# Rotary keys and queries: half-heads in two column tiles instead of 32-row swapped reads, in a hybrid Fourier and windowed-attention encoder

## The chip, the cores and the metric

One core of a Trainium2 chip runs the whole kernel. The metric is the device time of one execution in microseconds (us); of several runs the median counts. The kernel before takes 2726.4 us (median of three, 2724.59 to 2726.91).

## The reference, cut to what matters

One encoder layer on two batches, 512 and 256 positions, which share all weights; the kernel treats them as T = 768 columns. D is 2048. The part that the change touches is the projection `z = h @ w_in`, the rotation of q and k, and the way into the attention:

```python
h = rmsnorm(x, ln_mix_g)
z = h @ w_in                      # 2048 -> 1024 fourier | 1024 q | 256 k | 256 v
of = fourier_mix(zf, w_fourier)   # 8 groups x 128 channels: Re(2-D DFT), then a map per group
def apply_rope(x, cos, sin):      # x: (B, S, heads, 64)
    half = HEAD_DIM // 2
    x1, x2 = x[..., :half], x[..., half:]
    rot = jnp.concatenate([-x2, x1], axis=-1)
    return x * c + rot * s        # c, s: cos and sin per position, the same for all heads
q = apply_rope(q, cos, sin); k = apply_rope(k, cos, sin)   # 16 q heads, 4 k heads
oa = window_attention(q, k, v, attn_sink)   # each token sees +-128 positions, sink logit per head
x = x + concat([rmsnorm(of), rmsnorm(oa)]) @ w_out
x = x + relu(rmsnorm(x) @ w_up)**2 @ w_down            # then a final rmsnorm
```

All data are float32. TensorE takes a rounded form, so each operand is split in a high and a low part and each product is made of three matmuls (high x high, high x low, low x high). "Split" below means: ScalarE (ACT) writes the high part, VectorE (DVE) subtracts it from the source and writes the low part.

## The kernel before, in words

The stages follow one another on TensorE (PE): transposing and norming x, the v projection, the Fourier group's projection, then a stage that we call the pieces, then attention interleaved with the output projection, then the MLP, which is two thirds of the time.

The stage of the pieces makes the columns of k and q. There are five pairs of 256 columns (`cols`), and each pair is four pieces of 512 rows of `w_in`: 20 pieces, 0 to 19, of 48 matmuls each. Pair 0 holds the four key heads; pairs 1 to 4 hold query groups 0 to 3 (four heads that share a key head). A piece's weights come by a 512 KB load on SP's queue (`wload`, L79) into `raw`, two buffers; `split` makes `wh` (L69, ACT) and `wl` (L70, DVE). A pair's products lie in four PSUM tiles `pz` (L818), which is all there are: the next pair's first matmul waits until ACT has copied the tiles out (`zs`, L826). While PE works on pieces 0 to 10, the other engines carry out the Fourier group's DFT steps; `todo` holds work that is emitted after a certain piece or half piece.

The rotation goes by DRAM. ACT copies a pair's result to `zs`, writes it to `zk_d` or `zq_d` in three writes: 64 rows per head, and again its first 32 rows as rows 64 to 95. `rows2` reads rows 0 to 63 of two heads as `rx` and rows 32 to 95 as `ry`, in two halves of 384 positions, so `ry` has the halves of the heads swapped. Such a read stands in the code as

```python
nc.sync.dma_start(out, src[:, d : d + 64, t0])     # 2 heads x 64 rows x 384 positions
```

`rotate` (L677 on POOL, L678 and L679 on DVE) gives x cos + y sin. `keys` splits the rotated keys into `kdh`, `kdl` (L695, L697), which hold each key group in both halves of the partitions. `queries` splits the rotated queries into `rh`, `rl` (L72, L73) and writes them to DRAM (`qr_d`, L710, L711). 16 such jobs (4 for keys, 12 for query groups 0 to 2) are queued at pieces 10 to 18, and group 3 is read back and rotated in the attention.

Attention has 24 units (6 blocks of 128 positions x 4 groups). `load_q` reads a unit's queries from DRAM into `rx` (L723, L724), `split_q` copies them to `qs` (L740), and PE makes the scores `s` (L862) from `kdh`, `kdl` and `qs`. Between them lie matmuls of the output projection (`pm`, L1051, L1053). The order there is a list of events with times in steps of one eighth of a projection slot, units 7.37 steps apart (`pace`); the engines' queues are laid out in that order. Up to the end of piece 18 the queues of ACT, DVE, POOL and SP get their order from a scheduler, and PE's order is that of the code.

Of the kernel before, what the change touches and what calls it, by code (L numbers as in the profile page):

```python
# [20 lines left out]
P = 128  # L21
# [19 lines left out]
def hybrid_encoder(ctx: ExitStack, tc: tile.TileContext, a: dict):  # L41
# [74 lines left out]
    zk_d = [dpool.tile([2, 96, T], F32, tag=f"zk{i}", name=f"zk{i}") for i in range(2)]  # L116
    zq_d = [dpool.tile([4, 96, T], F32, tag=f"zq{i}", name=f"zq{i}") for i in range(NKV)]
    qr_d = [[dpool.tile([2 * P, T], F32, tag=f"q{c}{i}", name=f"q{c}{i}") for c in "hl"] for i in range(NKV - 1)]
# [79 lines left out]
    with ExitStack() as ph:  # L198
# [339 lines left out]
        zp = ph.enter_context(tc.tile_pool(name="zp", bufs=2, reuse_waits="tile"))  # L538


# [107 lines left out]
        def fourier_norm():  # L648
            ps_r = pp.tile([P, 512], F32, tag="f", bufs=4, name="ps_r")
            for m in range(NM):  # L650
                nc.tensor.matmul(ps_r[:, m : m + 1], ssf[:, m * P : (m + 1) * P], ones[:, 0:1], start=True, stop=True)
            rsqrt_of(r1[:], ps_r[:, :NM], FG * P, NM)
            fctx.close()


        kt = {}

        def open_attention():
            kp = kt["kp"] = kctx.enter_context(tc.tile_pool(name="kp", bufs=1, side="right", reuse_waits="tile"))
            for name, shape, src in (  # L660
                ("mask", [P, 384], a["c_mask"]), ("cosr", [P, T], a["c_cos"]), ("sinr", [P, T], a["c_sin"]),
                ("sink", [P, 64], a["attn_sink"].partition_broadcast(P)),
            ):
                kt[name] = kp.tile(shape, F32, tag=name, name=name)
                nc.sync.dma_start(kt[name][:, : src.shape[1]], src)
            for name in ("cosr", "sinr"):
                nc.vector.tensor_tensor(out=kt[name][:], in0=kt[name][:], in1=rb[:], op=ALU.mult)
            kt["kdh"] = kp.tile([P, NKV, T], F32R, tag="kdh", name="kdh")
            kt["kdl"] = kp.tile([P, NKV, T], F32R, tag="kdl", name="kdl")

        def rotate(x, y, t0, engine=nc.gpsimd):

            shape = x.shape
            cb, sb = (
                kt[c][: shape[0], t0].rearrange("p (o t) -> p o t", o=1).to_broadcast(shape) for c in ("cosr", "sinr")
            )
            engine.tensor_tensor(out=y, in0=y, in1=sb, op=ALU.mult)  # L677
            nc.vector.tensor_tensor(out=x, in0=x, in1=cb, op=ALU.mult)  # L678
            nc.vector.tensor_tensor(out=x, in0=x, in1=y, op=ALU.add)  # L679

        def rows2(src, t0):

            x, y = (kt["kp"].tile([P, 1, 512], F32, tag=c, name=c, bufs=n)[:, :, :HALF] for c, n in (("rx", 2), ("ry", 2)))
            for out, d in ((x, 0), (y, 32)):
                nc.sync.dma_start(out, src[:, d : d + 64, t0])
            return x, y

        def keys(i, t0, x, y):
            rotate(x, y, t0)
            x = x[:, 0, :]  # L690
            kdh, kdl = kt["kdh"], kt["kdl"]
            for r in range(2):
                g, rs = 2 * i + r, slice(r * HD, (r + 1) * HD)
                for h in (slice(0, 64), slice(64, 128)):
                    nc.scalar.activation(kdh[h, g, t0], x[rs], AF.Copy)  # L695
                for h in (slice(0, 64), slice(64, 128)):
                    nc.vector.tensor_tensor(out=kdl[h, g, t0], in0=x[rs], in1=f32(kdh[rs, g, t0]), op=ALU.subtract)  # L697

        def queries(g, i, t0, x, y):

            rs = slice(i * P, (i + 1) * P)
            rotate(x, y, t0)
            x = x[:, 0, :]
            if g < 2:
                hi = kt["kp"].tile([P, 512], F32R, tag="qs", name="rh", bufs=2)[:, :HALF]
            else:
                hi = kt["kp"].tile([P, HALF], F32R, tag="rl", name="rh", bufs=2)[:]
            lo = kt["kp"].tile([P, HALF], F32, tag="rl", name="rl", bufs=2)
            split(hi, lo[:], x, HD ** -0.5)
            nc.scalar.dma_start(qr_d[g][0][rs, t0], f32(hi))  # L710
            nc.scalar.dma_start(qr_d[g][1][rs, t0], lo[:])  # L711
# [4 lines left out]
        def load_q(u):  # L716
            b, g = units[u]
            t0 = slice(b * P, (b + 1) * P)
            x = kt["kp"].tile([P, 4, P], F32, tag="rx", name="rx", bufs=2)
            state[u] = {"x": x}  # L720
            if g < NKV - 1:
                rows = lambda src: src[:, t0].rearrange("(h d) t -> d h t", d=HD)
                nc.sync.dma_start(x[0:64], rows(qr_d[g][0]))  # L723
                nc.sync.dma_start(x[64:128], rows(qr_d[g][1]))  # L724
                return
            y = kt["kp"].tile([P, 4, P], F32, tag="ry", name="ry", bufs=2)
            for out, d in ((x, 0), (y, 32)):
                nc.sync.dma_start(out[0:64], zq_d[g][:, d : d + 64, t0].rearrange("h d t -> d h t"))
            state[u]["y"] = y

        def rotate_q(u):
            b, g = units[u]
            if g == NKV - 1:
                rotate(state[u]["x"][:HD], state[u].pop("y")[:HD], slice(b * P, (b + 1) * P), nc.vector)

        def split_q(u):
            x = state[u].pop("x")
            qs = state[u]["qs"] = kt["kp"].tile([P, 4, P], F32R, tag="qs", name="qs", bufs=2)
            if units[u][1] < NKV - 1:
                nc.scalar.activation(qs[:], x[:], AF.Copy)  # L740
                return
            nc.scalar.activation(qs[0:64], x[0:64], AF.Copy, scale=HD ** -0.5)
            nc.vector.scalar_tensor_tensor(
                out=qs[64:128], in0=x[0:64], scalar=HD ** -0.5, in1=f32(qs[0:64]), op0=ALU.mult, op1=ALU.subtract
            )
# [16 lines left out]
        jobs = [(keys, (i,), zk_d[i][:], s) for i in range(2) for s in range(2)]  # L762
        jobs += [(queries, (g, i), zq_d[g][2 * i : 2 * i + 2], s) for g in range(NKV - 1) for i in range(2) for s in range(2)]
        got = {}

        def job_load(i, src, s):
            got[i] = rows2(src, slice(s * HALF, (s + 1) * HALF))

        for i, (fn, args, src, s) in enumerate(jobs):
            t = 10.5 + 0.5 * i  # L770
            after(t - 0.5, lambda i=i, src=src, s=s: job_load(i, src, s))
            after(t, lambda i=i, fn=fn, args=args, s=s: fn(*args, slice(s * HALF, (s + 1) * HALF), *got.pop(i)))
        for u in range(2):
            after(18.5 + 0.5 * u, lambda u=u: (load_q(u), split_q(u)))
        after(18.5, lambda: load_of(0, [kt["kp"].tile([P, 4, P], F32, tag="ry", name="ofr", bufs=2) for _ in range(2)]))
        dst = [zk_d[i][:] for i in range(2)]
        dst += [zq_d[i // 2][i % 2 * 2 : i % 2 * 2 + 2] for i in range(8)]
        cols = [2048, 1024, 1280, 1536, 1792]
# [11 lines left out]
        def piece_split(p):  # L790
            if p < n_in:
                in_w[p] = wsplit(in_raw.pop(p))
# [11 lines left out]
        for piece in range(n_in):  # L804
            pair, j = divmod(piece, 4)
            if piece == 19:
                last.enter_context(tc.manual_schedule(engines={mybir.EngineType.Activation, mybir.EngineType.DVE}))
# [4 lines left out]
            for c in range(2):  # L812
# [9 lines left out]
                if j == 3:  # L822
                    zs = zp.tile([P, T], F32, tag="zs", name="zs")
                    for s in range(2):
                        hs = slice(s * HALF, (s + 1) * HALF)
                        nc.scalar.copy(zs[:, hs], ps[c][s][:, :HALF])  # L826
                    queue, to = nc.gpsimd if piece == n_in - 1 else nc.scalar, dst[2 * pair + c]
                    queue.dma_start(to[:, :64], zs[:])
                    for r in range(2):
                        queue.dma_start(to[r, 64:], zs[64 * r : 64 * r + 32])  # L830
# [8 lines left out]
        last.close()  # L839
# [160 lines left out]
    t_w, t_of, t_xc, t_y, t_oa, t_oa0, t_oa1, t_rot, t_split = 42.05, 7.45, -0.05, 2.7, 67, 4.2, 4.95, 5.8, 9  # L1000
# [15 lines left out]
    for u in range(len(units)):  # L1016
# [53 lines left out]
    with tc.manual_schedule(engines={mybir.EngineType.SP, mybir.EngineType.Activation, mybir.EngineType.DVE, mybir.EngineType.Pool}):  # L1070
# [14 lines left out]
        run_events(1e9)  # L1085
    att.close()
# [673 lines left out]
def _constants():  # L1760
# [20 lines left out]
        "c_cos": f(np.concatenate([c, c, c, c], 0)),  # L1781
        "c_sin": f(np.concatenate([-sn, sn, -sn, sn], 0)),
# [33 lines left out]
```

## Time and profile before

| | us |
|---|---|
| median of three runs | 2726.4 |
| profiled execution, its own time | 2724.45 |
| its span | 2722.7 |
| PE busy in the span | 2588.2 (95%) |
| DVE busy | 1805.1 (66%) |
| ACT busy | 1123.4 (41%) |
| POOL busy | 255.0 (9%) |
| PE busy from 300 to 503: pieces 11 to 19, up to the first score | 87.15 of 203 |

The profiled execution takes 1.75 us beyond its span. In the rows of the trace the times are microseconds from the start of the span; a row of PE's timeline has the start, the length, and in brackets the idle time ahead of it and what ended that. "<-" between two tile names reads "made from". SPq is the queue of SyncE, in which loads stand in order: a load that waits for a free buffer holds up all loads behind it.

### The profile page before, as it was taken

How to read it: one execution, taken by the hardware profiler on the slowest of the kernel's cores; microseconds unless marked ns; L12 is line 12 of the kernel's file. 1: busy time of each engine (PE TensorE's matmuls, PEld its weight loads, DVE VectorE, ACT ScalarE, POOL GpSimd, SP SyncE). 2: the span in 40 equal slices, each digit the busy share in tenths (PEclk: the TensorE clock that was granted, in tenths of full speed). 3: DMA queues.
4: the chain of work that ended last, by engine and by line, in shares of the span. 5: the costliest groups of instructions: out<-in, count | busy, mean ns of one | idle time of the engine just before them, and what ended most of it. 6: DMA issues, size and time to landing. Idle time of an engine off the chain costs nothing.

```text
span 2722.7 us, 35114 instructions
## 1 busy us (share of the span) xinstructions
PE 2588.2 (95%) x13580; PEld 2366.8 (87%) x13580; DVE 1805.1 (66%) x2230; ACT 1123.4 (41%) x1613; POOL 255.0 (9%) x359
## 2 busy tenths in 40 slices
PE   9999735599999999999999999999999999999998
PEld 9999735488888999999999999988888888888887
DVE  7955221577775655655677777767775774777687
ACT  6534210477643333333344444443333333333335
POOL 1002200222421010100000000020000000000000
PEclk9999867799999999999999999999999999999999
DMA  7954222534457445445666666686553481555264
GB/s 255 312 199 132 88 85 92 180 115 130 159 191 237 152 166 180 171 148 204 226 213 221 230 214 222 213 304 230 172 181 117 157 302 57 174 179 175 85 209 155
DMA packets 270008, 492.30 MB, mean 181 GB/s; under 512 B 20641, under 2 KB 164561, under 8 KB 268689
## 3 DMA queue, kind: packets, MB, share of 16 engines
q1 hardware_dynamic: 200624, 322.84, 36.9%
q10 hardware_dynamic: 55216, 115.18, 11.2%
q0 software_dynamic: 14000, 52.05, 5.6%
q8 instruction: 106, 1.74, 0.3%
q14 instruction: 62, 0.50, 0.1%
HBM read 361.92 MB, written 128.06 MB: 180 GB/s over the span
## 4 chain that ended last, share of the span: by engine, by line
PE 89%; DMA 7%; DVE 2%; SPq 0%; issue 0%; POOL 0%; ACT 0%; DVEq 0%; POOLq 0%; ACTq 0%
PE pu L1197 34%; PE pd L1632 33%; PE pm L1051 8%; PE p L268 4%; PE pz L818 3%; DMA rx<-zq 3%; DMA ry<-zq 2%; PE pv L391 1%; DMA ry<-zk 1%; PE s L862 1%; PE t L919 1%; PE o L938 1%; DMA rx<-zk 1%; PE pe L633 0%; PE pa L612 0%
## 5 line engine op out<-in xcount | busy, mean ns | idle before, releaser
L1197 PE MATMUL pu<-xf,wh 128*128 128x384 f32 x3072 | 780.2, 334 | 0.0
L1197 PEld LDWEIGHTS pu<-xf,wh 128*128 128x128 f32 x3072 | 553.9, 188 | 1.5 <-ACT o L1215 1.3
L1632 PE MATMUL pd<-wl,sh 128*128 128x512 f32 x1332 | 517.7, 389 | 0.0
L1632 PE MATMUL pd<-wh,sh 128*128 128x512 f32 x1332 | 517.7, 389 | 0.0
L1632 PE MATMUL pd<-wh,sl 128*128 128x512 f32 x1332 | 517.5, 389 | 0.0
L1197 PE MATMUL pu<-xf,wl 128*128 128x384 f32 x1536 | 513.1, 334 | 0.0
L1609 ACT ACTIVATE wh<-rd 128x1024 fp32r<-128x1024 f32 x200 | 202.4, 1054 | 522.2 <-PE pd L1632 414.3
L1619 DVE TENSOR_TENSOR wl<-rd,wh 128x1024 fp32r<-128x1024 f32 x200 | 236.1, 1221 | 226.3 <-ACT wh L1609 225.6
L1177 ACT ACTIVATE wh<-ur 128x1024 fp32r<-128x1024 f32 x160 | 170.0, 1063 | 382.5 <-PE pu L1197 207.4
L1632 PEld LDWEIGHTS pd<-wh,sl 128*128 128x128 f32 x1332 | 249.9, 188 | 52.1 <-DVE sl L1620 0.3
L1632 PEld LDWEIGHTS pd<-wl,sh 128*128 128x128 f32 x1332 | 250.0, 188 | 51.9
L1632 PEld LDWEIGHTS pd<-wh,sh 128*128 128x128 f32 x1332 | 250.0, 188 | 51.6
L1197 PEld LDWEIGHTS pu<-xf,wl 128*128 128x128 f32 x1536 | 288.3, 188 | 0.0
L1183 DVE TENSOR_TENSOR wl<-ur,wh 128x1024 fp32r<-128x1024 f32 x160 | 195.4, 1221 | 75.8 <-ACT wh L1177 75.7
L1218 DVE TENSOR_TENSOR o<-pu,o 128x768 f32<-128x768 f32 x160 | 152.8, 955 | 122.8 <-PE pu L1197 114.9
L1602 DVE TENSOR_TENSOR rd<-rd 128x1024 f32<-128x1024 f32 x112 | 131.7, 1217 | 0.0
L1197 PE MATMUL pu<-xs,wh 128*128 128x384 f32 x512 | 129.8, 334 | 0.0
L818 PE MATMUL pz<-xf,wh 128*128 128x384 f32 x320 | 72.5, 349 | 58.5 <-ACT zs L826 58.5
L1177 ACT ACTIVATE wh<-sx 128x1024 fp32r<-128x1024 f32 x64 | 67.9, 1062 | 130.5 <-PE pu L1197 104.3
L268 PE MATMUL p<-xs,wh 128*128 128x384 f32 x448 | 113.9, 334 | 0.0
L818 PEld LDWEIGHTS pz<-xf,wh 128*128 128x128 f32 x320 | 58.8, 197 | 59.5 <-ACT zs L826 59.3
L1620 DVE TENSOR_TENSOR sl<-sr,sh 128x768 fp32r<-128x768 f32 x111 | 105.5, 950 | 0.0
(283 smaller groups left out, 3970.8 us busy)
## 6 DMA issues: line engine op xcount, KB each, us to landing
rd<-in_w_down SPq DMA_DIRECT2D x176, 512.0 KB
ur<-in_w_up SPq DMA_DIRECT2D x128, 512.0 KB
sr<-sd SPq DMA_DIRECT2D x95, 384.0 KB
pd<-o ACTq DMA_DIRECT2D x60, 384.0 KB
o<-pd POOLq DMA_DIRECT2D x60, 384.0 KB, 6.0
sd<-sm ACTq DMA_DIRECT2D x60, 384.0 KB
raw<-in_w_in SPq DMA_DIRECT2D x38, 512.0 KB
raw<-in_w_out SPq DMA_DIRECT2D x32, 512.0 KB
```

The lines of the kernel that those rows point to most:

```text
L268: nc.tensor.matmul(ps7[bank, g, r][:, :HALF], l[:, i, r * P : (r + 1) * P], x[:, o, 4 * e + i, :], start=(opens and e == 0 and i == 0 and ...
L818: nc.tensor.matmul(ps[c][s][:, :HALF], w[:, i, cs], whole[j // 2][s][o][:, 4 * (j % 2) + i, :], start=first and n == 0, stop=stop and n == 2,)
L1051: nc.tensor.matmul(ps, l(k), w[:, k % 2, :], start=(k == 0 and n == 0), stop=(k == 7 and n == 2))
L1177: nc.scalar.activation(wh[:], raw[:], AF.Copy)
L1183: nc.vector.tensor_tensor(out=wl[:], in0=raw[:], in1=f32(wh[:]), op=ALU.subtract)
L1197: nc.tensor.matmul(ps[:, t, :HALF], w[:, i, t * P : (t + 1) * P], xb[:, o, i, :], start=(s == first_of[bank] and i == 0 and n == 0), stop= ...
L1218: nc.vector.tensor_tensor(out=o, in0=src, in1=o, op=ALU.add)
L1602: add = lambda x, y, op: nc.vector.tensor_tensor(out=x[:], in0=x[:], in1=y[:], op=op)
L1609: nc.scalar.activation(wh[:], t[:], AF.Copy)
L1619: nc.vector.tensor_tensor(out=wl[:], in0=t[:], in1=f32(wh[:]), op=ALU.subtract)
L1620: nc.vector.tensor_tensor(out=sl[:], in0=sr[:], in1=f32(sh[:]), op=ALU.subtract)
L1632: nc.tensor.matmul(o, l[:, q, ts], w[:, ns], start=(j == j0 and (q, t) == (0, 0)), stop=(j == j1 and (q, t) == (1, 2)),)
```

## The change

The weight columns of a pair are permuted when the pieces are split: the high and low parts are written with the column order (d, head) instead of (head, d). So column tile c = 0 of a pair (128 rows of the product) holds the first halves of its four heads, and c = 1 the second halves, at the same row. Then the swapped partner of a row lies in the other tile on the same partition, and rotation needs no swapped read: z0 cos - z1 sin, z1 cos + z0 sin. The tables `c_cos` and `c_sin` are laid out accordingly.

The order of the pairs is now keys, group 2, group 0, group 1, group 3 (`cols`, `order`). Pairs 0 and 1 still go by DRAM (`zs_d`, one write for each tile, one read of 768 KB). Pairs 2, 3 and 4 are copied from PSUM straight into the tile that is rotated. The rotation works in three steps of 256 positions (`cross` on POOL, `turned` on DVE, `parts` on ACT and DVE), and the high and low parts of keys and queries are written to `kr_d` and `qr_d`. The keys come back by four loads of 768 KB (`load_k`); `load_q` reads the queries straight into `qs`, without the copy by ACT. Pair 4 is rotated in the attention's events, and a unit's queries are loaded 1.5 steps after the time of the unit two before it (`t_lq`).

```diff
-        jobs = [(keys, (i,), zk_d[i][:], s) for i in range(2) for s in range(2)]
-        jobs += [(queries, (g, i), zq_d[g][2 * i : 2 * i + 2], s) for g in range(NKV - 1) for i in range(2) for s in range(2)]
...
-        cols = [2048, 1024, 1280, 1536, 1792]
+        cols = [2048, 1536, 1024, 1280, 1792]
+        order = [None, 2, 0, 1, 3]
+        for pair, t, ahead in ((0, 10.5, 10), (2, 11.5, None), (1, 13, 12), (3, 15, None)):
+            if ahead is not None:
+                after(ahead, lambda pair=pair: load_z(pair))
+            for s in range(3):
+                after(t + s // 2 * 0.5, lambda pair=pair, s=s: cross(pair, s))
+                after(t + 0.5 + s // 2 * 0.5, lambda pair=pair, s=s: (turned(pair, s), parts(pair, s)))
+        after(13, load_k)
...
+        def z_tile(pair):
+            zt[pair] = (zo["p"] if pair in (2, 3) else kt["kp"]).tile([P, 2, T], F32, tag="zs", name="zs")
+
+        def load_z(pair):
+            z_tile(pair)
+            nc.sync.dma_start(zt[pair][:], zs_d[pair][:].rearrange("(b p) t -> p b t", p=P))
+
+        def cross(pair, s):
+            ts = slice(s * 256, (s + 1) * 256)
+            y = ys[pair, s] = kt["kp"].tile([P, 2, 256], F32, tag="zy", name="zy", bufs=2)
+            for b in range(2):
+                nc.gpsimd.tensor_tensor(out=y[:, b], in0=zt[pair][:, 1 - b, ts], in1=kt["sinr"][:, ts], op=ALU.mult)
+
+        def turned(pair, s):
...
+            nc.vector.tensor_tensor(out=z, in0=z, in1=cb, op=ALU.mult)
+            for b, op in enumerate((ALU.subtract, ALU.add)):
+                nc.vector.tensor_tensor(out=z[:, b], in0=z[:, b], in1=y[:, b], op=op)
+
+        def parts(pair, s, when=lambda dt, fn: fn()):
...
+            put = lambda o, x: nc.scalar.dma_start(out[o][:, ts].rearrange("(b p) t -> p b t", p=P), x)
...
+                nc.scalar.activation(hi[:], z, AF.Copy, scale=scale)
+                low = lambda: nc.vector.scalar_tensor_tensor(
+                    out=z.bitcast(F32R), in0=z, scalar=scale, in1=f32(hi[:]), op0=ALU.mult, op1=ALU.subtract
+                )
+            put(0, f32(hi[:]))
+            when(t_zl, low)
+            when(t_zp, lambda: put(1, z))
+
+        def load_k():
+            for o, c in enumerate(("kdh", "kdl")):
+                for h in (slice(0, HD), slice(HD, P)):
+                    nc.sync.dma_start(f32(kt[c][h]), kr_d[o][:].rearrange("(d h) t -> d h t", h=NKV))
...
-            x = kt["kp"].tile([P, 4, P], F32, tag="rx", name="rx", bufs=2)
+            qs = kt["kp"].tile([P, 4, P], F32R, tag="qs", name="qs", bufs=2)
+            for o in range(2):
+                nc.sync.dma_start(f32(qs[o * HD : (o + 1) * HD]), qr_d[g][o][:, t0].rearrange("(d h) t -> d h t", h=4))
...
-                in_w[p] = wsplit(in_raw.pop(p))
+                raw = in_raw.pop(p)
+                wh, wl = in_w[p] = [wpool.tile([P, 4, 256], F32R, tag=f"w{c}", name=f"w{c}", bufs=4) for c in "hl"]
+                hi, lo = (w[:].rearrange("p i (d h) -> p i h d", h=4) for w in (wh, wl))
+                split(hi, lo, raw[:].rearrange("p i (h d) -> p i h d", h=4))
...
-            at(t - 3, lambda u=u: load_q(u + 2))
-            at(t - 3 + t_rot, lambda u=u: rotate_q(u + 2))
-            at(t - 3 + t_split, lambda u=u: split_q(u + 2))
+            at(t + t_lq + (u == 1), lambda u=u: load_q(u + 2))
...
+    t_cross, t_turn, t_parts = (0, 0.1, 3.2), (3, 4.6, 6.5), (5.9, 7.6, 9.5)
+    for s in range(3):
+        at(t_cross[s], lambda s=s: cross(len(cols) - 1, s))
+        at(t_turn[s], lambda s=s: turned(len(cols) - 1, s))
+        at(t_parts[s], lambda s=s: parts(len(cols) - 1, s, later))
```

From piece 19 on, all four queues are now laid out in the order of the code, and the last copies out of PSUM (pair 4, c = 1) go to DVE.

SP's queue, from the load of the sine table on, stood so before; `zk_78` and `zk_79` are the DRAM tiles of the keys, `zq_80` that of query group 0, and `raw` is a weight piece:

```order
L665 DMA sinr<-in_c_sin 128x768
L665 DMA sink<-in_attn_sink 128x16
L685 DMA rx<-zk_78 128x1x384
L685 DMA ry<-zk_78 128x1x384
L685 DMA rx<-zk_78 128x1x384
L685 DMA ry<-zk_78 128x1x384
L79 DMA raw<-in_w_in 128x4x256
L685 DMA ry<-zk_79 128x1x384 x2
L685 DMA rx<-zk_79 128x1x384
L685 DMA ry<-zq_80 128x1x384
L685 DMA rx<-zk_79 128x1x384
L685 DMA rx<-zq_80 128x1x384
```

It now stands so, up to the first two output-projection weights; `zs_78` is pair 0 in DRAM (keys), `zs_79` pair 1 (group 2), `kh` and `kl` are the rotated keys' parts:

```order
L664 DMA sinr<-in_c_sin 128x768
L664 DMA sink<-in_attn_sink 128x16
L678 DMA zs<-zs_78 128x2x768
L79 DMA raw<-in_w_in 128x4x256 x2
L720 DMA kdh<-kh 64x3072
L678 DMA zs<-zs_79 128x2x768
L720 DMA kdh<-kh 64x3072
L720 DMA kdl<-kl 64x3072 x2
L79 DMA raw<-in_w_in 128x4x256 x2
L79 DMA raw<-in_w_out 128x2x512
```

The 32 reads that stood among the weight loads are gone from the queue, and six loads of 768 KB stand there instead; two weight pieces stand behind the four loads of the keys.

ACT's queue before, around the copies that free PSUM for the last pair (here `zq_82` is group 2's DRAM tile, `qh_84` to `ql_87` are rotated parts of groups 0 and 1):

```order
L69 ACTIVATE wh<-raw 128x1024
L72 ACTIVATE rh<-rx 128x384
L710 DMA qh_84<-rh 128x384
L711 DMA ql_85<-rl 128x384
L72 ACTIVATE rh<-rx 128x384
L710 DMA qh_86<-rh 128x384
L826 COPY zs<-pz 128x384 x2
L711 DMA ql_87<-rl 128x384
L828 DMA zq_82<-zs 2x64x768
L830 DMA zq_82<-zs 32x768 x2
L826 COPY zs<-pz 128x384 x2
```

ACT's queue now at the copies of pair 3, which free PSUM for pair 4 (`qh_86` and `ql_87` are now the parts of group 2, which is pair 1):

```order
L69 ACTIVATE wh<-raw 128x4x4x64
L709 ACTIVATE zh<-zs 128x512
L704 DMA qh_86<-zh 128x2x256
L709 ACTIVATE zh<-zs 128x512
L704 DMA ql_87<-zs 128x2x256
L704 DMA qh_86<-zh 128x2x256
L704 DMA ql_87<-zs 128x2x256
L709 ACTIVATE zh<-zs 128x512
L704 DMA qh_86<-zh 128x2x256
L704 DMA ql_87<-zs 128x2x256
L815 COPY zs<-pz 128x384 x4
L69 ACTIVATE wh<-raw 128x4x4x64
```

Before, the copies stood between single jobs' rotations; now all four stand behind the whole of pair 1's splitting and writing.

More of the change, by code (lines that the diff above doesn't have):

```diff
@@ L653, in fourier_norm @@
             fctx.close()
+            zo["p"] = ph.enter_context(tc.tile_pool(name="zo", bufs=1, reuse_waits="tile"))
+        zo = {}
         kt = {}
@@ L665, in open_attention @@
                 nc.sync.dma_start(kt[name][:, : src.shape[1]], src)
[L666 to L705, printed above, removed]
-            else:
[L707 to L711, printed above, removed]
+            for t in (kt["cosr"][:], kt["sinr"][:]):
+                nc.vector.tensor_tensor(out=t, in0=t, in1=rb[:], op=ALU.mult)
@@ L718, in load_q @@
             t0 = slice(b * P, (b + 1) * P)
-            x = kt["kp"].tile([P, 4, P], F32, tag="rx", name="rx", bufs=2)
[L720 to L745, printed above, removed]
+            qs = kt["kp"].tile([P, 4, P], F32R, tag="qs", name="qs", bufs=2)
+            state[u] = {"qs": qs}
+            for o in range(2):
+                nc.sync.dma_start(f32(qs[o * HD : (o + 1) * HD]), qr_d[g][o][:, t0].rearrange("(d h) t -> d h t", h=4))
         todo = {}
@@ L761, in hybrid_encoder @@
         after(10, open_attention)
-        jobs = [(keys, (i,), zk_d[i][:], s) for i in range(2) for s in range(2)]
-        jobs += [(queries, (g, i), zq_d[g][2 * i : 2 * i + 2], s) for g in range(NKV - 1) for i in range(2) for s in range(2)]
[L764 to L772, printed above, removed]
-        for u in range(2):
[L774 to L777, printed above, removed]
-        cols = [2048, 1024, 1280, 1536, 1792]
+        cols = [2048, 1536, 1024, 1280, 1792]
[7 more added lines that the diff above has]
+        after(13, load_k)
+        for u in range(2):
+            after(17 + 0.5 * u, lambda u=u: load_q(u))
+        after(17, lambda: load_of(0, [kt["kp"].tile([P, 4, P], F32, tag="zy", name="ofr", bufs=2) for _ in range(2)]))
         n_in = 4 * len(cols)
@@ L806, in hybrid_encoder @@
             if piece == 19:
[L807 removed]
+                last.enter_context(tc.manual_schedule(engines={mybir.EngineType.SP, mybir.EngineType.Activation, mybir.EngineType.DVE, mybir.EngineType.Pool}))
             if j == 0:
@@ L822, in hybrid_encoder @@
                 if j == 3:
-                    zs = zp.tile([P, T], F32, tag="zs", name="zs")
-                    for s in range(2):
[L825 to L830, printed above, removed]
+                    if c == 0 and pair >= 2:
+                        z_tile(pair)
+                    if pair < 2:
+                        zs = fp.tile([P, T], F32, tag="zs", name="zs", bufs=2)
+                        put = [zs[:, :HALF], zs[:, HALF:]]
+                    else:
+                        put = [zt[pair][:, c, s * HALF : (s + 1) * HALF] for s in range(2)]
+                    for s in range(2):
+                        (nc.vector.tensor_copy if piece == n_in - 1 and c == 1 else nc.scalar.copy)(put[s], ps[c][s][:, :HALF])
+                    if pair < 2:
+                        nc.scalar.dma_start(zs_d[pair][c * P : (c + 1) * P, :], zs[:])
                     if piece == n_in - 1 and c == 0:
@@ L1085, in hybrid_encoder @@
         run_events(1e9)
+    last.close()
     att.close()
```

31 lines of the change are left out of this document (22 added, 9 removed).

## The prediction

> **What bounds the kernel now.** I read the page first: its 40 slices, then the chain that ended last.
>
> ```profile
> PE   9999735599999999999999999999999999999998
> PEclk9999867799999999999999999999999999999999
> PE 89%; DMA 7%; DVE 2%; SPq 0%; issue 0%; POOL 0%; ACT 0%; DVEq 0%; POOLq 0%; ACTq 0%
> ```
>
> A slice is 68 us. PE is full everywhere but in slices 5 to 8, which are 272 to 545 us; and the chain leaves PE for the DMA's 7% and DVE's 2% of the span, 245 us. PE's waits from 300 to 520 us name what it lacks (total us, times, longest):
>
> ```profile
> PE pz L818 <- ACT zs L826: 58.5, 2, 43.9
> PE s L862 <- ACT qs L740: 32.5, 1, 32.5
> PE pz L818 <- ACT wh L69: 16.5, 2, 10.9
> PE pz L818 <- DVE wl L70: 8.6, 1, 8.6
> ```
>
> Together 116.1 us ahead of the first score. ACT and DVE are named, but the busy times by stretch (busy and count of PE, PEld, DVE, ACT, POOL, then granted clock, DMA share, GB/s) say that they too were waiting:
>
> ```profile
> 300.00:503.00 203.00, 87.15 (x451) 84.19 (x449) 43.59 (x72) 28.30 (x48) 20.28 (x20) 0.71 0.29 98
> 340.00:350.00 10.00, 10.00 (x60) 10.00 (x59) 0.00 (x0) 0.00 (x0) 1.02 (x1) 1.00 0.14 53
> 440.00:450.00 10.00, 0.17 (x1) 0.00 (x0) 1.03 (x2) 0.48 (x2) 1.81 (x2) 0.71 0.13 50
> 500.00:510.00 10.00, 3.83 (x10) 2.95 (x11) 3.56 (x7) 6.30 (x12) 3.75 (x6) 0.50 0.94 270
> ```
>
> No engine is busy for a quarter of the 203 us except PE. In the two stretches from 340 and 440 the DMA share is 0.14 and 0.13, about 2 of 16 engines, at some 50 GB/s. The chain in order of time (start, length) shows whose transfers those are:
>
> ```profile
> 303.36 0.42 SPq L665
> ...
> 311.35 21.74 DMA ry<-zk
> ...
> 498.00 1.84 DMA ql<-rl
> ...
> 501.14 4.54 DMA rx<-ql
> ```
>
> The swapped reads, 192 KB each, hold this chain for up to 22 us at a time, while a write of the same size takes 1.84 and a query load of 128 KB, with DMA at 0.94, takes 4.54. Copies from PSUM stand on ACT behind rotations that wait for these reads, so PE cannot begin the next pair.
>
> The Trainium skill gives a reason ("DMA: Bandwidth & Descriptors", section "Why a DMA increments its semaphore by 16 and not by 1"): the number of engines is the largest one up to 16 that divides the outermost dimension of both sides, so a read whose outer dimension is the 2 heads gets two. The shares of 0.13 and 0.14 agree with it; that the new transfers, with 64 or 128 outermost, spread further is shown by no run here.
>
> **What goes.** PE's timeline gives what the pieces would take unhindered:
>
> ```profile
> 302.29 0.94 PE L818 MATMUL pz<-xs,wh 128*128 128x384 f32 x4
> 310.70 0.85 PE L818 MATMUL pz<-xf,wh 128*128 128x384 f32 x4
> 329.66 1.71 PE L818 MATMUL pz<-xf,wh 128*128 128x384 f32 x4 [14.64 <-ACT zs L826]
> 335.35 0.85 PE L818 MATMUL pz<-xf,wh 128*128 128x384 f32 x4
> 344.71 0.85 PE L818 MATMUL pz<-xs,wh 128*128 128x384 f32 x4
> 503.28 0.58 PE L862 MATMUL s<-kdl,qs 128*128 128x256 f32 x1 [32.55 <-ACT qs L740]
> 506.97 0.79 PE L1051 MATMUL pm<-wh,ofh 128*128 128x512 f32 x1 [2.90 <-ACT ofh L69]
> ```
>
> Piece 11 runs from 302.29 to 310.70. From 335.35 to 344.71 stand nine groups of six matmuls, 1.04 each, so a piece of 48 takes 8.32. Pieces 12 to 19 then end at 310.70 + 8 x 8.32 = 377.3, where the first score could start: 503.28 - 377.3 = 126.0 us is the most that the pieces can give. It is more than the 116.1 of waits because PE also restarts slowly: the 18 matmuls from 329.66 to 335.35 take 5.7 where 3.1 would do, 2.6 lost after a wait of 14.64.
>
> **What comes instead.** The durations I scale from these groups (busy us, mean ns) and two rows of DVE:
>
> ```profile
> L677 POOL TENSOR_TENSOR ry<-ry,sinr 128x384 f32<-128x384 f32 x16 | 16.2, 1011 | 172.2 <-DMA ry<-zq 132.4 <-issue 20.4 <-DMA ry<-zk 19.5
> L678 DVE TENSOR_TENSOR rx<-rx,cosr 64x512 f32<-64x512 f32 x1 | 0.7, 677 | 0.0
> L606 DVE TENSOR_TENSOR ft<-pa,ft x8: 417/424/425, 196.4 to 285.4; 128x256 f32<-128x256 f32 x8
> L743 DVE SCALAR_TENSOR_TENSOR qs<-rx,qs x6: 684/851/958, 528.1 to 700.0; 64x512 fp32r<-64x512 f32 x6
> L740 ACT ACTIVATE qs<-rx x18: 615/621/635, 502.6 to 688.3; 128x512 fp32r<-128x512 f32 x18
> 309.27 0.96 DVE L667 TENSOR_TENSOR sinr<-sinr,rb 128x768 f32<-128x768 f32 x1 [2.04 <-DMA sinr<-in_c_sin]
> ```
>
> A step of 256 positions costs two POOL products of 128x256 (between 1.0 x 256/384 = 0.67 and 1.01; I take 0.8, so 1.6), on DVE 0.68 + 2 x 0.42 = 1.5 for turning and 0.68 (keys) or 0.85 (queries) for the low part, on ACT 0.62. So a pair is 3 x 2.4 = 7 us of DVE and 5 of POOL, against 33 us that PE needs for a pair: no engine is the bound, only latency can be.
>
> *Keys.* The load of pair 0 is issued where `rx<-zk` was, at 304.4. The sine table's 384 KB were issued at 303.36 and there at 309.27, 5.9 us; 768 KB may land after 8.6, at 313. Then come POOL's first 1.6, DVE's 3 x 2.2, one weight's low part (1.2), the first products of pair 2 on DVE (1.1), and ACT and DVE waiting for each other once or twice: the last part is written at about 326. PE needs the weights behind this in DVE's queue only for piece 15 at 335.7. No stall.
>
> *Pair 1* has the one tile that pair 0 had, so its load waits until the keys' last write has landed (2.5 us, between the 1.84 above and 4.54): issued 328.5, landed after some 6.5 (between 4.54 and 8.6) at 335. Its rotation takes 1.6 + 3 x 2.4 + a weight's low part 1.2 + 0.6 + puts, to 346.8. In ACT's queue the copies of pair 3 stand behind it, and piece 16 needs the first of them; it would start at 310.70 + 4 x 8.32 = 344.0 and starts at 347.3: 3.3 us of new stall.
>
> *The permuted split.* The high and low parts are now written with a stride of four elements. Before has no such operation. Below it lies DVE's plain piece, above it a reduction that reads with a stride and takes 1074 where a plain product of as many elements takes 677, 1.6 times; ACT's write at a stride of two elements shows no penalty:
>
> ```profile
> L70 DVE TENSOR_TENSOR wl<-raw,wh 128x1024 fp32r<-128x1024 f32 x40 | 48.8, 1225 | 16.9 <-ACT wh L69 16.9
> L69 ACT ACTIVATE wh<-raw 128x1024 fp32r<-128x1024 f32 x40 | 41.9, 1053 | 29.5 <-PE p L268 12.4 <-DMA wf<-in_w_fourier 7.1 <-PE pz L818 5.3
> L990 DVE TENSOR_REDUCE sr<-cx x1: 1074/1074/1074, 749.9 to 749.9; 128x128 f32<-128x512 f32 x1
> L635 ACT COPY of<-pe x8: 614/616/638, 208.3 to 296.2; 128x512 f32<-128x512 f32 x8
> 250.00:300.00 50.00, 50.00 (x332) 50.00 (x331) 24.72 (x55) 22.32 (x53) 12.48 (x9) 1.00 0.33 106
> ```
>
> I take the dear end, since the reduction is the only row of DVE with a stride: 0.7 us on DVE and as much on ACT per piece. Two pieces lie in pair 1's way, which makes 3 us; the stall at piece 16 is 6.3. In the Fourier stage DVE is busy for 24.72 of 50 and ACT for 22.32, so the ten pieces there cost between 0 and 7 us (0.7 each, if nothing hides them); I take 1.
>
> The Trainium skill speaks against this edit ("Advanced Engine Details and Errata", section "SBUF Cachelines"): lines are 16 bytes, and an access that meets a new line each time is slowed. Here each element lies 16 bytes from the last. The strided reduction agrees in kind and ACT's write at 8 bytes doesn't touch it; by the rule the sum is the one I take, and without it 3 to 4 us less.
>
> *Start of attention.* With a slow restart after a wait of 6 us (I take 1.9, less than the 2.6 after 14.64) the first score comes at 377.3 + 6.3 + 1.9 = 385.5, so 117.8 us earlier. Its loads are there: behind pair 1's load stand three of the keys' (at 5 to 8 us each done by 350 to 360), then the weights of pieces 18 and 19, the first of which PE needs at about 369, and the first queries. Today's start loses 2.90 for `ofh` and about 3 to the clock (0.76 over the first 20 us, so 4.8 at most). Both can go; but DVE gets pair 4's 7 us into the first 20, less 2.9 (three products of 0.68 and a split of 0.85) that unit 3 needs no more.
>
> ```profile
> 503.00:523.00 20.00, 16.82 (x71) 13.81 (x72) 12.09 (x36) 11.54 (x28) 5.63 (x9) 0.76 0.61 187
> 523.00:543.00 20.00, 20.00 (x108) 17.07 (x107) 16.13 (x51) 15.67 (x40) 6.49 (x12) 1.00 0.70 221
> 520.00:740.00 220.00, 217.33 (x1128) 182.88 (x1127) 168.90 (x485) 158.67 (x378) 67.04 (x105) 1.00 0.47 144
> ```
>
> 12.1 + 7.1 - 2.9 = 16.3 of 20 is as much as DVE carries from 523 to 543 with PE full. Between 5.9 gained and 3 lost I take 2 gained. The rest of attention has 2.7 us of idle PE in 220, so a lighter ACT there gives nothing; the MLP doesn't change.
>
> *Sum*, against the profiled execution: 2724.45 - 117.8 + 1 - 2 = 2605.65. Its time lies 1.95 under the median of the runs, so I predict 2607 for the median.
>
> **The rivals.**
> *No new stall.* Strided writes are free and pair 1's load lands in 3 us less: the score starts at 377.3, 126.0 gained. 2724.45 - 126 - 2 + 1.95 = 2598; with all 5.9 at the start, 2594.5. For it: the write of 192 KB in 1.84.
>
> *Later still.* The two loads of 768 KB take twice my estimate: 8.6 later for the first, 6.5 for the second. Pair 1 then ends 15 us later, and with it the copies and piece 16, whose slack is spent in my case already. 2607 + 15 = 2622; with 3 lost at the start of attention instead of 2 gained it is 2627. For it: when many loads meet, as from 500 to 510, DMA is full at 270 GB/s, and the landing times are the least sure of my numbers. Against it: a share of 0.29 over the stage.
>
> *It doesn't do what it says:* the new transfers stay on two engines. At 50 GB/s, 768 KB take 15.7 us. Keys' load, pair 1's load and four loads of keys, 94 us one behind the other with the key chain's 13 between, end at 304.4 + 94 + 13 = 411. The weights of piece 18 stand behind them (5 to land, 2.3 to split), then two pieces of 8.3: the score starts at about 435, and it is 2724.45 - 68 + 1.95 = 2658. Against it: writes with 128 rows outermost land in 1.84.
>
> *Slower than before: the query loads.* `load_q` now fills `qs` itself, of which there are two, so a load can only be issued when PE is done with the unit two before. From 1.5 steps to the next but one's score at 2 x 7.37 - 4.5 are 8.74 steps. A unit takes (700.0 - 528.1)/20 = 8.6 us by the first and last `qs` of group 3, so a step is 1.17 and the window 10.2 us. 22 units load in this way; the gain is gone when each waits (2726.4 - 2607)/22 = 5.4 us, that is from a landing of 15.6 us on; at 17 us it is 2607 + 22 x 6.8 = 2757. Against it: 4.54 in the busiest moment.
>
> **How the numbers follow.** What a measurement can tell from no change is about 0.2%, 5.5 us. My case 0.60; no new stall 0.13; later still 0.18; two engines 0.04; query loads 0.05, four fifths of it slower. The range, 2596 to 2628, holds the first three but for their edges; the last two are left out. Faster 0.95, within 0.2% 0.01, slower 0.04.
>
> **What would show it.** Right: the waits of `pz` for `zs` and of `s` for `qs` vanish from the list but for 6 us at piece 16; the first score at 385; loads of `zs` in 5 to 9 us; the DMA share above 0.3 while they run; `wl` at about 1.9 us a piece. Wrong: a share of 0.13 under the new loads; `s` waiting for `qs` in the attention; PE waiting for `ah`, `al` or `wl` before 300, where it is full now.

## The result and the profile after

The changed kernel takes 2603.7 us (median of four runs, 2601.49 to 2604.47) against 2726.65 us before: a ratio of 0.9549 with a 95% interval of 0.9533 to 0.9566, so 122.9 us less. 2607 was predicted, in a range of 2596 to 2628. The profiled execution takes 2604.47 us, its span is 2602.6.

From the page of the changed kernel: PE's slices, and the chain that ended last by engine:

```profile
PE   9999989999999999999999999999999999999998
PE 95%; DVE 2%; DMA 1%; ACT 1%; issue 0%; POOL 0%; ACTq 0%; DVEq 0%; POOLq 0%; SPq 0%
```

The hole in slices 5 to 8 is closed but for one slice at 8 tenths, and the chain has 1% of DMA where it had 7%. PE's waits from 300 to 420 us in the changed kernel (three more are 0.3 us or less):

```profile
PE pz L802 <- ACT zs L815: 9.4, 1, 9.4
PE pm L1042 <- DVE ofl L70: 1.3, 1, 1.3
```

One wait of 9.4 us stands ahead of the first score where four groups made 116. PE's timeline has it at piece 16, the first piece of pair 4; piece 11 begins at 302.47, 0.18 later than before, and the first score is at 389.23:

```profile
302.47 0.94 PE L802 MATMUL pz<-xs,wh 128*128 128x384 f32 x4
...
353.77 1.71 PE L802 MATMUL pz<-xf,wh 128*128 128x384 f32 x4 [9.45 <-ACT zs L815]
...
359.06 0.86 PE L802 MATMUL pz<-xf,wh 128*128 128x384 f32 x4
...
389.23 0.28 PE L848 MATMUL s<-kdl,qs 128*128 128x256 f32 x1
```

So 114.05 us are gained by the first score (503.28 before). The 18 matmuls behind the wait, from 353.77 to 359.06, take 5.29 us where 3.12 would do, so the slow restart costs 2.2. The first and the last score, by the rows of that tile before and after (min, median, max in ns, then first and last start), give the next share:

```profile
L862 PE MATMUL s<-kdl,qs x96: 274/285/582, 503.3 to 706.5; 128*128 128x256 f32 x64, 128*128 128x384 f32 x32
L848 PE MATMUL s<-kdl,qs x96: 274/281/421, 389.2 to 588.1; 128*128 128x256 f32 x64, 128*128 128x384 f32 x32
```

203.2 us became 198.9, so 4.3 more. The span is 120.1 us shorter; the remaining 1.8 lie behind the last score, and no run was made to find their cause. The stretch of the pieces, in the columns of the prediction's table by stretch, then the later part of it alone:

```profile
300.00:386.00 86.00, 76.55 (x434) 75.93 (x433) 45.35 (x59) 26.23 (x32) 28.25 (x26) 0.94 0.72 212
324.00:378.00 54.00, 44.55 (x246) 44.14 (x245) 30.12 (x41) 15.56 (x18) 15.51 (x15) 0.91 0.88 250
```

The DMA share is 0.72 where it was 0.29, and from 324 to 378 it is 0.88. This is the number that the experiments turn on. The chain (start, length) names two transfers behind the wait, and SP's queue the large loads that were issued around them:

```profile
324.33 7.21 DMA kl<-zs
...
331.60 10.21 DMA zs<-zs
```

```profile
324.01 0.53 SPq L720 DMA_DIRECT2D kdh<-kh  x1
...
332.02 0.51 SPq L720 DMA_DIRECT2D kdh<-kh  x1
332.58 15.85 SPq L720 DMA_DIRECT2D kdl<-kl  x2
```

The keys' last write (256 KB) takes 7.21 us and pair 1's load (768 KB) 10.21. One of the keys' four loads is issued just ahead of the write, two more just behind pair 1's load, and the fourth 16 us later.

### The profile page after: what moved, and what is told of

Read it like the earlier page. It is cut to its first block, busy times and chain, and to the rows that moved or that the text cites. A ratio compares the mean times of both kernels' runs of the same rounds, so it can differ in the third digit from the quotient of the medians.

```text
span 2602.6 us, 34971 instructions
## 1 busy us (share of the span) xinstructions
PE 2579.5 (99%) x13580; PEld 2360.6 (91%) x13580; DVE 1808.6 (69%) x2208; ACT 1124.5 (43%) x1574; POOL 264.9 (10%) x367
## 4 chain that ended last, share of the span: by engine, by line
PE 95%; DVE 2%; DMA 1%; ACT 1%; issue 0%; POOL 0%; ACTq 0%; DVEq 0%; POOLq 0%; SPq 0%
PE pu L1187 35%; PE pd L1622 35%; PE pm L1040 10%; PE pz L802 5%; PE p L268 4%; PE pv L391 1%; PE o L924 1%; PE s L848 1%; PE t L905 1%; DMA raw<-in_w_in 1%; PE pe L630 0%; PE pa L609 0%; PE ptx L137 0%; DMA zs<-zs 0%; POOL zy L687 0%
## 5 line engine op out<-in xcount | busy, mean ns | idle before, releaser
L1173 DVE TENSOR_TENSOR wl<-sx,wh 128x1024 fp32r<-128x1024 f32 x64 | 78.2, 1222 | 23.8 <-ACT wh L1167 23.6
L70 DVE TENSOR_TENSOR wl<-raw,wh 128x1024 fp32r<-128x1024 f32 x40 | 66.1, 1660 | 40.7 <-ACT wh L69 40.7
```

The source lines that it names most:

```text
L1173: nc.vector.tensor_tensor(out=wl[:], in0=raw[:], in1=f32(wh[:]), op=ALU.subtract)
```

## The experiments

**Was it the shape of the reads?** The kernel before, each read of two heads issued as two reads of one:

```diff
-                nc.sync.dma_start(out, src[:, d : d + 64, t0])
+                for r in range(2):
+                    nc.sync.dma_start(out[r * 64 : r * 64 + 64], src[r : r + 1, d : d + 64, t0].rearrange("o d t -> d o t"))
```

> The kernel before, with nothing changed but that each swapped read of two heads (2 x 64 x 384) is issued as two reads of one head (64 rows outermost). Theory (the reads were slow because their outer dimension of 2 kept them on two engines): each read lands in 3 to 6 us instead of 11 to 39, the DMA share between 300 and 400 us exceeds 0.4, PE's waits for zs, qs, wh and wl fall from 116 to under 50 us, and the time is 2610 to 2660 us. Rival (the round trip by DRAM and its 16 jobs are the cost, however the reads are shaped): above 2690 us.

2629.5 us (2628.49 to 2631.23), a ratio of 0.9648 (0.9633 to 0.9662) to before: 96 of the 123 us without any permutation. Its two largest groups of PE waits from 100 to 640 us, and the size and median time to land of the reads of the queries' pairs:

```profile
PE pz L819 <- ACT zs L827: 19.3, 2, 15.1
PE s L863 <- ACT qs L741: 5.6, 1, 5.6
...
ry<-zq SPq DMA_DIRECT2D x20, 96.0 KB, 3.8
rx<-zq SPq DMA_DIRECT2D x20, 96.0 KB, 3.9
```

The median read lands in under 4 us (the last column), the DMA share from 300 to 400 us is 0.57, and these waits, all that stand ahead of the first score, are 24.9 us in place of 116. The rival, that the round trip is dear in whatever shape, falls for most of the gain; 27 us are left for it, and no run here divides them further.

**The same in the changed kernel, the other way.** The DRAM tiles are laid out with 2 outermost. The read back of a pair becomes two reads of 384 KB with 2 outermost, one for each column tile (each write to them becomes two of 64 rows as well, which is not in this cut):

```diff
-    zs_d = [dpool.tile([2 * P, T], F32, ...
+    zs_d = [dpool.tile([2, 2, 64, T], F32, ...
-            nc.sync.dma_start(zt[pair][:], zs_d[pair][:].rearrange("(b p) t -> p b t", p=P))
+            for b in range(2):
+                nc.sync.dma_start(zt[pair][:, b : b + 1, :], zs_d[pair][:, b])
```

> The changed kernel, but the two DRAM tiles of pairs 0 and 1 are laid out so that each read back is two reads of 2 x 64 x 768 (384 KB), with 2 outermost. Theory (two engines): a read takes 9 to 17 us in place of 7 for pair 0 and 10 for pair 1, the stall ahead of piece 16 grows from 9.4 to 18 to 30 us, and the time is 2612 to 2628 us. Rival (the shape of a read does not matter, contention does): 2601 to 2606 us.

2631.3 us (2629.33 to 2634.0), past the upper end that was expected: 27.6 us for the reads of two pairs. Its chain and its wait at piece 16, POOL's products that waited for pair 1's second read, and a stretch in which only pair 0's second read was under way (the last three columns are granted clock, DMA share, GB/s):

```profile
303.86 19.12 DMA zs<-zs
...
343.36 15.17 DMA zs<-zs
...
PE pz L803 <- ACT zs L816: 36.9, 1, 36.9
```

```profile
368.05 2.54 POOL L688 TENSOR_TENSOR zy<-zs,sinr 128x256 f32<-128x256 f32 x3 [8.64 <-DMA zs<-zs]
316.00:322.00 6.00, 6.00 (x36) 6.00 (x35) 0.00 (x0) 0.00 (x0) 0.74 (x1) 1.00 0.13 52
```

The chain shows one read of each pair. Pair 0's second read takes 19.1 us, and pair 1's second is there only at 368.0, 24.7 us after the first was issued. In the changed kernel the two pairs' data were there 7.2 and 10.2 us after the issue; together they come about 27 us later here, the wait grows by 27.5, and the time by as much. A share of 0.13 at 52 GB/s, the mark of the kernel before, is back. Both ways the outer dimension of a read decides.

**The strided splits.** The weights are split as they lie, which leaves out the permutation:

```diff
-                hi, lo = (w[:].rearrange("p i (d h) -> p i h d", h=4) for w in (wh, wl))
-                split(hi, lo, raw[:].rearrange("p i (h d) -> p i h d", h=4))
+                split(wh[:], wl[:], raw[:])
```

> The changed kernel, with the weights split into contiguous high and low parts; it leaves out the permutation of the weight columns, so its heads are mixed. Theory (a strided split costs 0.8 to 1 us on each of two engines, and only the pieces in pair 1's way matter): wh back at 1.05 and wl at 1.22 us, PE full from 250 to 300 as it is with the stride, 1 to 4 us less in all, 2599.5 to 2602.5 us. Rival (the splits also slow the Fourier stage): 8 us less or more, under 2596 us.

2602.2 us (2600.26 to 2604.95), ratio 0.9548 (0.9533 to 0.9562): within what the theory expected, but no difference from the changed kernel that these runs can tell. The Fourier stage's rows (160 to 300 us) of the changed kernel, then of this one:

```profile
L69 ACT ACTIVATE wh<-raw 128x1024 fp32r<-128x1024 f32 x14 | 28.9, 2063 | 15.0 <-PE pz L802 7.2 <-PE p L268 3.9 <-DMA zf<-z 3.8
L70 DVE TENSOR_TENSOR wl<-raw,wh 128x1024 fp32r<-128x1024 f32 x14 | 28.4, 2031 | 19.2 <-ACT wh L69 19.2
```

```profile
L70 DVE TENSOR_TENSOR wl<-raw,wh 128x1024 fp32r<-128x1024 f32 x14 | 17.1, 1225 | 11.4 <-ACT wh L69 11.3
L69 ACT ACTIVATE wh<-raw 128x1024 fp32r<-128x1024 f32 x14 | 14.8, 1056 | 21.0 <-PE p L268 10.3 <-DMA wf<-in_w_fourier 7.1 <-PE pz L801 3.4
```

The stride costs ACT 1.0 us and DVE 0.8 a piece, and none of it shows in this kernel's time: the wait at piece 16 is 9.6 without it.

**What holds piece 16: ACT's order?** Pair 3's copies go ahead of pair 1's splits on ACT:

```diff
-        for pair, t, ahead in ((0, 10.5, 10), (2, 11.5, None), (1, 13, 12), (3, 15, None)):
+        for pair, t, ahead in ((0, 10.5, 10), (2, 11.5, None), (1, 15, 12), (3, 16, None)):
...
+            if piece == 15:
+                last.enter_context(tc.manual_schedule(engines={mybir.EngineType.Activation}))
```

> The changed kernel, with pair 3's copies out of PSUM ahead of pair 1's splits in ACT's queue (pair 1 queued two pieces later, ACT in the code's order from piece 15 on). Theory (the only wait left is that of piece 16 for these copies, 9.4 us and a slow clock of 2 to 3 us behind it): the wait is gone, the first score comes at 377 to 379 instead of 389.2, and the time is 2590 to 2594 us. Rival (pair 1's late load holds PE elsewhere, by the weights of pieces 18 and 19 or the queries of the first units): the wait turns up there, and the time is 2599 to 2604 us.

2602.8 us (2600.4 to 2603.88): the rival's time, but not at the place that it named. PE still waits 7.3 us at piece 16. The chain of this kernel:

```profile
334.15 17.15 DMA ql<-zs
...
351.36 0.49 ACT zs L817
```

The copies now wait for a write. Pairs 2 and 3 share one tile (`zo`), and pair 2's last 256 KB, issued at 334.15, land 17 us later; the median write of the keys' low parts took 2.3 with less beside it. Beside pair 1's load and two weight pieces, three of the keys' four loads are issued within 2 us of that write, and the keys are needed only at 377. Whether they are what crowds it, the next experiment tests.

**Or the keys' loads?** They are put behind pair 1's load and the last weights in SP's queue:

```diff
-        after(13, load_k)
+        after(15, load_k)
...
+            if piece == 12:
+                last.enter_context(tc.manual_schedule(engines={mybir.EngineType.SP}))
```

> The changed kernel, with the four loads of the keys put behind pair 1's load and the last weight pieces in SP's queue (load_k queued at piece 15, SP in the code's order from piece 12 on). ACT's order is left as the scheduler makes it. Theory (3 MB of key loads, issued from 324 us on, fill the DMA engines and hold up the keys' last write, pair 1's load and pair 2's last write; these landings, not ACT's order, cause the 9.4 us ahead of piece 16): the keys' last write lands in 2 to 4 us in place of 7.2, pair 1's load in 5 to 7 in place of 10.2, PE waits under 3 us, and the time is 2590 to 2596 us. Rival (the loads are only moved to where the weights or the first queries wait for them): a wait of s for kdl or qs, or of pz for wh or wl, of 6 us or more; 2598 to 2606 us.

2599.2 us (2598.47 to 2599.41). The time is the rival's, but the wait of 6 us or more that the rival needs appeared nowhere; the landings are the theory's. Pair 1's load, which waits for the keys' last write (issued at 325.19), could be issued 2.1 us behind it, and landed in about 5 us:

```profile
327.32 0.37 SPq L678 DMA_DIRECT2D zs<-zs  x1
...
zs<-zs SPq DMA_DIRECT2D x2, 768.0 KB, 5.0
PE pz L804 <- ACT zs L817: 3.0, 1, 3.0
```

The keys' loads are now issued from 344.90 on. So they were what had held both transfers up. The first score came at 383.0. What is left of the wait belongs to ACT's order: a weight's strided high part (2.00 us) ends just ahead of the copies.

```profile
345.41 2.00 ACT wh L69
347.41 0.33 ACT zs L817
```

Run again beside the changed kernel on one chip:

> The changed kernel as it is, beside the other two on one chip: 2601 to 2606 us by every theory.

> The kernel with the keys' loads moved alone, beside the changed one on one chip. Theory: 4 to 6 us under the changed kernel (its first score was 6.2 us earlier in the trace). Rival: within 2 us of it.

2603.8 us (2601.41 to 2604.64) for the changed kernel and 2598.2 (2597.49 to 2599.23) with the keys last: 5.5 us, and no run of the one reaches the other. The ratios to before are 0.9553 (0.954 to 0.9566) and 0.9534 (0.9521 to 0.9547). The two measurements with the keys last agree to 1 us, and no version has a lower median; but the last of the orders below has the same ratio to before, so the runs can't rank these two.

**Both edits, and where their gain goes.**

> The same, and pair 3's copies ahead of pair 1's splits in ACT's queue. Theory (landings are the cause, ACT's order adds the rest): PE has no wait over 1 us ahead of the first score, which comes at 377 to 379 us; 2589 to 2593 us, at most 4 us under the kernel with the keys' loads moved alone. Rival (ACT's order matters for itself once landings are early): 5 us or more under that kernel.

2600.0 us (2598.97 to 2601.14). PE has no wait in the pieces, and the first score comes at 378.1, 0.8 after the 377.3 that the prediction worked out as the earliest; but it is not faster than the keys' loads moved alone. PE's one large wait is now at the start of attention:

```profile
PE pm L1044 <- DVE zs L819: 7.6, 1, 7.6
```

DVE's copies stand behind the low part of a weight of the output projection, which comes late. The chain shows why:

```profile
348.14 14.35 DMA qh<-zh
...
370.11 3.99 DMA qh<-zh
374.17 0.56 SPq L731
...
376.99 6.26 DMA raw<-in_w_out
383.27 1.06 ACT wh L69
```

A write of pair 1's queries beside the keys' loads took 14.35 us, which put off all that follows on ACT. In SP's queue the weight stands behind the first queries (L731); their tile `qs` shares its two buffers with `zh`, so their load waited until the write issued at 370.11 had landed, and the weight was issued only at 376.99. SP's queue stood still for these 5.2 us, and the DMA share from 362 to 374 us is 0.61: the queue's order held the weight, and not the DMA engines alone.

Two more versions tried to get round the wait, one with the keys between the weights of pieces 18 and 19 (`after(14, load_k)`):

> The kernel with both edits, but the keys' four loads now stand between the weights of pieces 18 and 19, so that they run from 333 us on instead of 342. Theory (the 7.6 us that PE waits at the start of attention in the kernel with both edits come from 3 MB of keys beside piece 19's weights and pair 1's writes, and go when the keys run earlier): the first score at 378 to 381, no wait over 3 us ahead of or behind it, 2589 to 2594 us. Rival (from 330 to 375 the transfers fill the DMA engines, so that any order makes someone wait): a wait of 4 us or more for pair 2's last write, for piece 19's weights or at the start of attention; 2596 to 2602 us.

2605.3 us (2603.93 to 2606.35), above both ranges, but by the rival's mechanism: pair 2's last write lands after 18.1 us and piece 16 waits 9.5 again.

```profile
334.90 18.11 DMA ql<-zs
```

The other has the last copies ahead of that weight on DVE (`if piece == n_in - 1 and c == 1: piece_split(piece + 3)`):

> The kernel with both edits (keys' loads after piece 19's weights, pair 3's copies early on ACT), and the last copies out of PSUM stand on DVE ahead of the third output-projection weight instead of behind it. Theory (the 7.6 us at the start of attention were the wait of the first projection matmul for those copies behind a late weight): the wait falls to 1 to 4 us, the weight itself being late by the same crowded transfers; 2593 to 2597 us. Rival (the full DMA engines make the same time be lost at that weight): 2598 to 2601 us, with a wait of 5 us or more for it.

2599.4 us (2597.89 to 2600.4), the rival's time and its place: PE's first projection matmul waits 5.7 us for `ofh`, which ACT makes behind the high part of the same late weight.

```profile
PE pm L1044 <- ACT ofh L69: 5.7, 1, 5.7
376.89 5.56 DMA raw<-in_w_out
...
382.48 1.06 ACT wh L69
383.53 0.53 ACT ofh L69
```

The weight is again issued behind the first queries, at 376.89.

From 324 to 378 us the DMA share is 0.88 in the changed kernel, 0.88 with the keys last and 0.78 with both edits:

```profile
324.00:378.00 54.00, 54.00 (x314) 53.95 (x312) 30.96 (x43) 16.94 (x21) 16.44 (x15) 1.00 0.78 225
```

Six orders of the same transfers gave 2598 to 2605 us, and in each of them PE waited for some landing or for what stood behind one. That the bytes alone set this bound is not shown. Neither an order with that weight ahead of the first queries was tried, nor a version with fewer bytes (the keys are loaded twice, once for each half of the partitions).

**The slower rival.** Each unit's queries are loaded 6 steps later (`t_lq` 7.5 in place of 1.5):

> The changed kernel, with each unit's queries loaded 6 steps later (t_lq 7.5 in place of 1.5), so that the window from issue to the first score that needs them is 2.74 steps or 3.2 us instead of 10.2. It measures the rival of the prediction by which the query loads set the pace. Theory (a load of 2 x 128 KB lands in 3 to 5 us): scores wait for most of 22 loads, 0.3 to 2 us each, and the time is 2608 to 2650 us. If loads land within 3 us: 2601 to 2606 us, and the window was never near.

2624.2 us (2623.04 to 2628.14), 20.5 more than the changed kernel and in the theory's range. But only four scores waited, not most of 22:

```profile
PE s L848 <- DMA qs<-ql: 16.2, 4, 4.2
```

In the changed kernel 22 such pairs of loads land in 3.1 and 3.2 us (medians from 395 to 600 us), about the 3.2 of the short window. The four were late by SP's queue. The first of them:

```profile
412.85 0.37 SPq L188 DMA_DIRECT2D ofr<-ofd  x1
...
413.91 0.61 SPq L731 DMA_DIRECT2D qs<-ql  x1
...
418.48 0.36 PE L848 MATMUL s<-kdl,qs 128*128 128x256 f32 x1 [4.22 <-DMA qs<-ql]
```

PE was ready at 414.26, 0.35 us after the second load's issue. At the other three the second load was issued 0.3 to 1.2 us ahead, each time right behind a load that had waited for its own buffer, and the score came 4.4 to 5.2 us after the issue. Slower matmuls add to the loss: the granted clock from first to last score is 0.95 here and 1.00 in the changed kernel. PE's scores in the changed kernel, with a window of 10.2, have no wait for `qs` at all.

## Why the prediction was right, point by point

The time was within 3.3 us of the forecast, and the case that was held likeliest came about: the swapped reads go, one smaller wait takes their place at piece 16, and attention starts a little better. That the number came so close is in part luck, as the last paragraph of this section shows. (The forecast's last step, 2605.65 + 1.95, is 2607.6 and was put down as 2607.)

*The reads on two engines* were the cause for 96 of 123 us by the first experiment, and doing them so again cost 27.6 by the second. The Trainium skill's rule on how many engines a transfer gets ("DMA: Bandwidth & Descriptors", section "Why a DMA increments its semaphore by 16 and not by 1") agrees with both, and with the share of 0.13 that came back in the second.

*377.3 as the earliest first score* was right to 0.8: 378.1 with both edits.

*The stall at piece 16* was predicted as 6.3 us and was 9.45 in the profiled execution, and the first score came at 389.23 instead of 385.5, 3.7 later. The step that was mis-sized is landing under load. The keys' last write was given 2.5 us and took 7.21; pair 1's load was given 6.5 and took 10.21. An earlier start gave a part back: pair 0's rotation began at 310.14 instead of 313, and the keys' last write was issued at 324.33 instead of 326. So pair 1's data were there at 341.8 instead of 335; 3 us of that came back as no weight's strided part stood in pair 1's way (below). The prediction took the loads one by one. It did not count that the first of the keys' loads, of no use before 377, runs beside the keys' last write, and two more beside pair 1's load. Putting them last brought the two landings to 2.1 and 5.0. The prediction also named one holder of pair 3's copies where there are two: ACT's order, and the tile that pair 2 still writes from.

*The strided splits* were taken at 0.7 us on each engine and cost 0.8 and 1.0. The 3 us that they were to add to pair 1's way are not in the time: without them the wait at piece 16 was 9.6, and the chain of the changed kernel has no weight's split between pair 1's landing and the copies. The 1 us in the Fourier stage was 0.18. The Trainium skill's rule on lines of 16 bytes ("Advanced Engine Details and Errata", section "SBUF Cachelines") agrees with the durations on both engines; of the 3 to 4 us of time that hung on it, the runs show nothing.

*The start of attention* was taken at 2 us gained and gave 4.3 up to the last score. The wait for `ofh` went, the granted clock over the first 20 us is 1.00 where it was 0.76, and DVE carried pair 4 beside its other work: PE waited 1.3 us for `ofl`.

The terms that were mis-sized cancel, and that is luck: the first score came 3.7 us later than forecast (2.7 when the 1 us of the Fourier stage, which the sum adds apart, is counted in), and some 4 more were gained behind it, 1.8 of them behind the last score, for which the prediction had no term. *No new stall* was wrong for the changed kernel, and none of the orders tried was without a wait of 3 us or more. *Later still* had the right mechanism, transfers that meet, at a quarter of its size. *Two engines* and *the query loads* did not happen.

## What to carry to other kernels

Look at the DMA share of a stretch in which everybody waits: 0.13 with loads outstanding meant 2 of 16 engines, and splitting each read at its outer dimension alone, a change of two lines, gave four fifths of what the whole rewrite gave. After such a repair the same stretch may be crowded: then estimate landings by what else is issued at that time, put the loads that are needed last behind the ones that someone waits for, and look at what stands in a queue behind a load that waits for its buffer. A wait for a buffer can have two holders, so undo one and look for the other before the gain is promised.

## What the runs showed of the hardware

DVE and POOL slowed each other down when both worked on SBUF tiles. In the changed kernel DVE's product of 128x512 took 1.21 us while POOL made `zy`, and 0.69 with POOL idle:

```profile
343.44 1.21 DVE L694 TENSOR_TENSOR zs<-zs,cosr 128x512 f32<-128x512 f32 x1 [4.01 <-POOL zy L687]
345.26 0.69 DVE L694 TENSOR_TENSOR zs<-zs,cosr 128x512 f32<-128x512 f32 x1 [0.62 <-POOL zy L687]
```

A product of POOL (128x256) took 0.73 us with DVE idle, and 3.80 with DVE busy through most of it, first with a split of 2.60 us:

```profile
310.14 0.73 POOL L687 TENSOR_TENSOR zy<-zs,sinr 128x256 f32<-128x256 f32 x1 [5.89 <-DMA raw<-in_w_in]
321.44 3.80 POOL L687 TENSOR_TENSOR zy<-zs,sinr 128x256 f32<-128x256 f32 x1
320.81 2.60 DVE L70 TENSOR_TENSOR wl<-raw,wh 128x1024 fp32r<-128x1024 f32 x1
```

And a split with a stride of 16 bytes on one operand or more took ACT 1.95 times and DVE 1.66 times as long as a contiguous one (2063 against 1056 ns, 2031 against 1225).
